# Attention by residue classes first, unit's columns fetched in phase A, attention norm in place, later norms by whole rows

## The chip, the core and the metric

The kernel runs on one core of one Trainium2 chip. The metric is the device time of one execution in microseconds; the median of the runs is compared. A second number is the time of one profiled execution, whose trace is read below.

## The reference, cut to what matters

Two sequences (prompt and sample) of 1024 tokens, 1024 features wide, pass through one encoder layer. Only what the change touches is shown.

```python
def encoder_layer(h, ...):
    z = rms_norm(h, g_mix) @ w_in                 # q, k, v (512 each) and u (512)
    att = attention_mixer(q, k, v, rel_bias)      # 8 heads of 64
    ssm = ssm_mixer(u, ...)                       # state-space part, then
                                                  # g * sigmoid(g @ w_glu + b_glu), the "unit"
    mix = concatenate([rms_norm(att, g_att_out), rms_norm(ssm, g_ssm_out)])
    h = h + mix @ w_out
    f = rms_norm(h, g_mlp)
    h = h + square(relu(f @ w_mlp1)) @ w_mlp2
    e = rms_norm(h, g_ple)
    h = h + sigmoid(e @ w_ple_gate) * (p_i @ w_ple_proj)
# at the end: rms_norm(h, g_final)
def attention_mixer(q, k, v, rel_bias):
    # three branches, windows (128, 512, 2048) at dilations (1, 4, 16); each gives
    # an output and the logarithm of its denominator, and these weigh the outputs
```

## The kernel before, in words

The kernel has three phases. **Phase A** norms the inputs, multiplies them by `w_in`, stores q, k, v and u in scratch memory, and runs the state-space part; the planner orders its instructions. **Phase B** (class `PhaseB`) is the attention, in an order written by hand for TensorE, VectorE and ScalarE: 64 steps, eight to a pair of heads, four pairs to a sequence. Each pair n has four blocks of contiguous windows (branch of dilation 1; tiles `q`, `k`, `v64`, statistics `sta`, output `ota`) and four blocks of residue classes modulo 4 (the two other branches together; tiles `qr`, `kr`, `vc`, statistics `stb`, output `otb`). `step(g)` does, for the block g and its neighbours, the scores (L783), bias and minimum (L807, VectorE), exponent (L815, ScalarE), transposes (L823), copies of these (L827) and products with v (L844), and copies the result with `put` (L852, L854). Before, blocks 0 to 3 of a pair are the windows and 4 to 7 the classes. `moved` (L888) exchanges `stb` between partitions into `sx` by four DMAs on GpSimd's queue; `joined` (L922) takes the statistics of both branches, works out their weights (L907 to L919), turns the outputs (L940), weighs them (L944), adds them (L947) and stores the tile `at` (L949). For the last pair `joined` runs after the loop, in one piece.

Between the steps, at four places of each, run other tasks as generators: `gelu` and `unit` of class `Glu` (the state-space part's end) and `att_norm` (L1096, the norm of the attention's output of the first sequence). `Glu` loads two columns of 512 values at its start (L965, L966), the unit's weights (L968), and `gelu` halves the columns on VectorE (L977) before it loads the first block of y (L982); GpSimd squares y (L986), VectorE goes on two steps later (L989). `att_norm` takes eight tiles of 128 tokens, one after another: product with gain and scale (L1114), four transposes (L1118), a high part by ScalarE (L1121) and the remainder by VectorE (L1122), each stored in scratch memory (L1125). The tag of the high parts has two buffers, that of the remainders one.

All loads and stores except `moved` go through SP's queue, in the order that the planner gives them. A new tile in a buffer waits until the tile before it has been read.

**Phase C** (class `PhaseC`) does `w_out`, the MLP and the PLE part for one sequence after the other, in split products (each operand as a high part and a remainder, three matmuls for one: L455 to L457; splits at L1168 and L1169, on ScalarE and on VectorE or GpSimd). `norm` (L1158) is called for four tiles at a time, twice before the MLP and twice before the PLE part, in each sequence. It uses `norm_to_act` (L523): squares and their sum on ScalarE (L519), the reciprocal root on VectorE (L419 to L428), the row scaled by it on ScalarE (L532), and for each of the 8 feature blocks of a group of two tiles two transposes (L537), a copy times the gain column on ScalarE (L540) and the remainder on VectorE (L541). Gains are columns (`gcol`, 1024 values of 4 bytes); the gain of the attention norm and the last norm are rows (`gvec`, tile `gbc`, one buffer). The last norm multiplies by row and scale in one VectorE operation (L1408).

Of the kernel before, what the change touches and what calls it, by code (L numbers as in the profile page):

```python
# [431 lines left out]
class Act:  # L432
# [12 lines left out]

    def rhs(self, k, th):
        return self.hi[k // 4, th][:, k % 4], self.lo[k // 4, th][:, k % 4]
# [75 lines left out]
def norm_to_act(nc, small, ps, tag, ident, act, T0, srcs, dst, gcol, nk, junks, group):  # L523

    r = rstd_rows(nc, small, srcs, nk * P, junks)
    last = None
    for t0 in range(0, len(srcs), group):
        ts = range(t0, min(t0 + group, len(srcs)))
        dsts = []
        for t in ts:  # L530
            dsts.append(dst(t))
            nc.scalar.activation(dsts[-1], srcs[t], AF.Copy, scale=r[:, t:t + 1])  # L532
        c = slice(P * ((T0 + t0) % 4), P * ((T0 + t0) % 4) + P * len(ts))
        for k in range(nk):
            pt = ps.tile([P, 4, P], F32, tag=tag, name="n_ps")
            for t in range(len(ts)):
                nc.tensor.transpose(pt[:, t], dsts[t][:, P * k:P * k + P], ident)  # L537
            hi, lo = (x[k // 4, T0 // 4][:, k % 4, c] for x in (act.hi, act.lo))
            pv = pt[:, 0:len(ts)].rearrange("p t c -> p (t c)")
            nc.scalar.activation(hi, pv, AF.Copy, scale=gcol[:, k:k + 1])  # L540
            last = nc.vector.scalar_tensor_tensor(lo, pv, gcol[:, k:k + 1], hi.bitcast(F32), op0=ALU.mult, op1=ALU.subtract)  # L541
    return last
# [127 lines left out]
class PhaseB:  # L670
# [6 lines left out]
    def __init__(self, nc, tc, ctx, early, ident, scr):  # L677
        self.nc, self.tc, self.ident, self.scr = nc, tc, ident, scr
        self.early = early

        def pool(name, bufs, **k):
            return ctx.enter_context(tc.tile_pool(name=name, bufs=bufs, reuse_waits="tile", **k))

        self.ld = [pool("Bl0", 1)]
        self.sp = pool("Bs", 7)
        self.ptp = pool("Bpt", 4)
        self.op = pool("Bo", 2)
        self.ap = pool("Ba", 1)
        self.sm = pool("Bsm", 2)
        self.ld.append(pool("Bl1", 1))  # L690
        self.ps_s = pool("Bps", 4, space=PSUM)
        self.ps_o = pool("Bpo", 1, space=PSUM)
        self.ps_t = pool("Bpt2", 2, space=PSUM)
        self.ps_x = pool("Bpx", 1, space=PSUM)
        self.tasks, self.busy, self.normed, self.place = [], False, False, 0
        self.pairs, self.pss, self.sbs, self.pts = {}, {}, {}, {}
# [22 lines left out]
    def load(self, n):  # L719
# [8 lines left out]
        with self.tc.high_priority(offset=FIRST_AHEAD if n == 0 else LOAD_AHEAD):  # L728
            q, k = (first([P, S], F32, "raw", nm) for nm in "qk")
            for t, nm in ((q, "zq"), (k, "zk")):  # L730
                nc.sync.dma_start(out=t, in_=scr[nm, s, p])
# [8 lines left out]
            v64 = ld.tile([P, 9, P], F32, tag="v64", name="v64")  # L740
            nc.sync.dma_start(out=v64, in_=zv.rearrange("(j m) e -> m j e", m=P))
            qr, kr = (ld.tile([P, 4, 256], F32, tag=nm, name=nm) for nm in ("qr", "kr"))
            for t, nm in ((qr, "zqr"), (kr, "zkr")):
                nc.sync.dma_start(out=t, in_=scr[nm, s, p])
            vc = ld.tile([P, 4, 2, P], F32, tag="vc", name="vc")
            for r in range(4):
                nc.sync.dma_start(out=vc[:, r], in_=zv[64:1088].rearrange("(f m r) e -> r m f e", m=P, r=4)[r])
        d = self.pairs[n] = dict(q=q, k=k, qr=qr, kr=kr, vc=vc, v64=v64, bt=bt)
# [12 lines left out]
    @staticmethod  # L761
    def cols(blk, u):
        return slice(64 if blk == u == 0 else 0, 192 if blk == 3 and u else 256)

    def scores(self, g):
# [6 lines left out]
        for u in range(2):  # L772
            w = self.cols(blk, u)
            for h in range(2):
                r = slice(64 * h, 64 * h + 64)
                if blk < 4:
                    i = 2 * b + u
                    ql = d["q"][r, P * i:P * i + P]
                    kr = d["k"][r, P * i - 64 + w.start:P * i - 64 + w.stop]
                else:  # L780
                    ql = d["qr"][r, b, P * u:P * u + P]
                    kr = d["kr"][r, b]
                self.nc.tensor.matmul(pss[h][:, u, w], ql, kr, start=True, stop=True)  # L783

    def stats(self, g, h, u):
        n, blk = g // 8, g % 8
        if blk < 4:
            st, i = self.some(n, "sta"), 2 * blk + u
            return [st[:, j, h, i:i + 1] for j in range(2)]
        st = self.some(n, "stb")  # L790
        return [st[:, blk - 4, j, h, u:u + 1] for j in range(2)]

    def reduced(self, g, h):
# [3 lines left out]
        for u in range(2):  # L797
            w = self.cols(blk, u)
            if blk < 4:
# [17 lines left out]
    def turn(self, g, h):  # L817
        sb = self.sbs.pop((g, h))
        self.pts[g, h] = pt = self.ps_t.tile([P, 4, P], F32, tag="pt", name="pt")
        for u in range(2):  # L820
            for kt in range(2):
                slot = 2 * u + kt if g % 8 < 4 else 2 * kt + u
# [7 lines left out]
    def values(self, g):  # L830
# [4 lines left out]
        if blk < 4:  # L835
# [12 lines left out]
    def put(self, g):  # L848
        n, blk = g // 8, g % 8
        b = blk % 4  # L850
        if blk < 4:
# [4 lines left out]
    def step(self, g, N=64):  # L856
# [18 lines left out]
        if on(g + 1):  # L875
            self.exponent(g + 1, 1)
            if g % 8 == 6:
                self.moved(g // 8)
# [43 lines left out]
    def joined(self, n, last=False):  # L922
# [3 lines left out]
        if not last:  # L926
            yield from self.at(3)
        ea, eb = yield from self.weights(n)
        at = self.ap.tile([P, 8, 2, 64], F32, tag="at", name="at")
# [24 lines left out]
class Glu:  # L954


    def __init__(self, nc, tc, ctx, io, ident, ones, scr, B):
# [6 lines left out]
        self.cols = self.one.tile([P, 8], F32, name="cols")  # L964
        nc.sync.dma_start(out=self.cols[:, 0:4], in_=io["b_glu"].rearrange("(f p) -> p f", p=P))  # L965
        nc.sync.dma_start(out=self.cols[:, 4:8], in_=io["g_ssm_out"].rearrange("(f p) -> p f", p=P))  # L966
# [5 lines left out]
    def gelu(self):  # L972
# [4 lines left out]
        nc.vector.tensor_scalar(self.cols, self.cols, 0.5, None, op0=ALU.mult)  # L977
# [118 lines left out]
def att_norm(nc, B, pool, g, io, scr, s):  # L1096
# [15 lines left out]
    for T, at in enumerate(ats):  # L1112
# [7 lines left out]
        hi, lo = (pool.tile([P, 4, P], F32R, tag="a" + x, name="ato", bufs=n) for x, n in (("h", 2), ("l", 1)))  # L1120
# [8 lines left out]
class PhaseC:  # L1129
# [23 lines left out]
    def gcol(self, src):  # L1153
        g = self.sm.tile([P, 8], F32, tag="gcol", name="gcol")
        self.nc.sync.dma_start(out=g, in_=src.rearrange("(k p) -> p k", p=P))
        return g

    def norm(self, h, gb, a, i):  # L1158

        a.half(i)  # L1160
        junks = [self.gp.tile([P, D], BF16, tag="junk", name="junk") for _ in range(4)]
        norm_to_act(self.nc, self.sm, self.pm1, "m1", self.ident, a, 4 * i, h[4 * i:4 * i + 4],
                    lambda t: self.sp.tile([P, D], F32, tag="s", name="ft"), gb, 8, junks, 2)
# [111 lines left out]
    def run(self, s, x, p, y, first=None):  # L1275
# [11 lines left out]
        gb = self.gcol(io["g_mlp"])  # L1287
# [13 lines left out]
        for ch in range(8):  # L1301
# [41 lines left out]
            else:  # L1343
# [26 lines left out]
                gb = self.gcol(io["g_ple"])  # L1370
# [42 lines left out]
def encoder_kernel(ctx, tc, io, y_prompt, y_sample):  # L1413
# [6 lines left out]
    m16 = c.tile([16, 16], F32, name="m16")  # L1420
    scr = {"u": tc.dram_tile([NG, 16, 8, 2, NCK], F32, name="u_scr"),
# [15 lines left out]
    with ExitStack() as ab:  # L1437
# [3 lines left out]
        with ExitStack() as as_:  # L1441
# [28 lines left out]
            M = Ssm(nc, tabs, ssmp, ps_gp, pk, ident, *ssm_in, m16, scr["u"], scr["y"])  # L1470
            M.step(0)
# [3 lines left out]
            A.qk(1, act, lambda p: M.step(5 + p))  # L1475
            A.v(1, act)
        right.close()
        with ExitStack() as bs:
# [3 lines left out]
            G = Glu(nc, tc, gs, io, ident, ones, scr, B)  # L1482
            bp = first = None
            for g in range(-3, 66):
                B.step(g)
                if bp is None and G.halves == 4 and g >= 40:
# [8 lines left out]
            place = 0  # L1495
# [3 lines left out]
            for _ in B.joined(7, True):  # L1499
                pass  # L1500
# [59 lines left out]
```

## Time and profile before

| what | us |
|---|---|
| median of 3 runs | 2791.08 (2786.3 to 2793.44) |
| the profiled execution | 2791.4 |
| its span, first to last instruction | 2789.6 |
| busy: TensorE | 2600.3 (93%) |
| busy: VectorE | 1583.1 (57%) |
| busy: ScalarE | 1190.6 (43%) |
| busy: GpSimd | 1129.4 (40%) |

In the rows, PE is TensorE, PEld its weight loads, DVE VectorE, ACT ScalarE, POOL GpSimd, SP the engine that issues the transfers. A row of a timeline has the start and the length in microseconds, the engine, the line, what was done, and in brackets how long the engine had been idle before and what released it. The granted clock is the share of TensorE's full speed.

### The profile page before, as it was taken

The page shows a single profiled execution, that of the slowest core. Times are in us where ns is not written, and L with a number is a line of the kernel's source. Part 1 is how long each engine was busy: PE and PEld are TensorE (multiplying, and loading weights), DVE is VectorE, ACT ScalarE, POOL GpSimd, SP SyncE. Part 2 cuts the span into 40 slices and gives each one's busy share as a digit, 9 for nine tenths or more (in the row PEclk, how much of TensorE's full clock was granted, in tenths as well). Part 3 has the DMA queues.
Part 4 walks back from the last instruction along what each step waited for, and adds up shares of the span by engine and source line. Part 5 has one row for each costly group of instructions (what it writes and reads, how often), then busy time and mean ns, then how long its engine had stood idle before and what let it go on. Part 6 is the DMA issues. An engine that isn't in the chain of part 4 may idle for free.

```text
span 2789.6 us, 33993 instructions
## 1 busy us (share of the span) xinstructions
PE 2600.3 (93%) x12206; PEld 2044.3 (73%) x12206; DVE 1583.1 (57%) x2923; ACT 1190.6 (43%) x2378; POOL 1129.4 (40%) x817
## 2 busy tenths in 40 slices
PE   6998878969997898999999999999999999999997
PEld 4866657755565686888788877787788888888776
DVE  4788775557776433475555574353356455457435
ACT  6433324236667444333333334533533333333452
POOL 1133343223331352464554464344344555455332
PEclk9999989989999898999999999999999999999999
DMA  8524453254447601122121222252111111111201
GB/s 280 150 78 121 157 165 115 91 173 150 150 130 267 195 31 32 48 72 72 42 68 42 64 91 64 84 204 72 53 54 53 46 42 57 61 53 46 72 16 61
DMA packets 271723, 266.67 MB, mean 96 GB/s; under 512 B 46897, under 2 KB 222001, under 8 KB 269505
## 3 DMA queue, kind: packets, MB, share of 16 engines
q1 hardware_dynamic: 270528, 264.36, 29.8%
q8 instruction: 96, 1.57, 0.2%
q14 instruction: 75, 0.61, 0.1%
q0 software_dynamic: 1024, 0.13, 0.0%
HBM read 194.55 MB, written 67.66 MB: 94 GB/s over the span
## 4 chain that ended last, share of the span: by engine, by line
PE 76%; DVE 12%; DMA 4%; ACT 4%; issue 2%; POOL 1%; SPq 0%; DVEq 0%; ACTq 0%; POOLq 0%
PE m L455 19%; PE m L457 19%; PE m L456 19%; PE glu L1014 2%; PE ag L455 2%; PE ag L457 2%; PE ag L456 2%; PE pss L783 1%; PE po L844 1%; PE n_ps L537 1%; PE pt L823 1%; DMA w<-in_w_mlp_dram 1%; PE s_pb L251 1%; DVE s_t L274 1%; ACT sb L815 1%
## 5 line engine op out<-in xcount | busy, mean ns | idle before, releaser
L1169 POOL TENSOR_TENSOR lo<-wr_b,hi 128x512 fp32r<-128x512 f32 x264 | 376.6, 1434 | 567.2 <-ACT hi L1168 552.5
L455 PE MATMUL m<-acth,hi 128*128 128x512 f32 x1024 | 403.9, 396 | 2.2 <-ACT hi L1168 2.2
L456 PE MATMUL m<-acth,lo 128*128 128x512 f32 x1024 | 403.2, 394 | 1.5 <-POOL lo L1169 1.5
L457 PE MATMUL m<-actl,hi 128*128 128x512 f32 x1024 | 403.1, 394 | 0.0
L1255 DVE TENSOR_TENSOR h<-h,m 128x512 f32<-128x512 f32 x448 | 288.3, 680 | 140.7 <-PE m L457 139.7
L456 PE MATMUL m<-hi,lo 128*128 128x512 f32 x912 | 354.8, 393 | 3.7 <-DVE lo L1169 3.7
L457 PE MATMUL m<-lo,hi 128*128 128x512 f32 x912 | 353.6, 394 | 0.3 <-POOL lo L1169 0.3
L455 PE MATMUL m<-hi 128*128 128x512 f32 x912 | 337.2, 396 | 4.8 <-DVE h L1255 3.6
L1168 ACT CAST hi<-wr_b 128x512 fp32r<-128x512 f32 x264 | 163.7, 621 | 410.1 <-PE m L456 375.9
L1169 DVE TENSOR_TENSOR lo<-hid,hi 128x512 fp32r<-128x512 f32 x200 | 185.1, 927 | 165.0 <-ACT hi L1168 165.0
L1169 POOL TENSOR_TENSOR lo<-w,hi 128x512 fp32r<-128x512 f32 x128 | 176.0, 1382 | 165.3 <-ACT hi L1168 164.0
L456 PEld LDWEIGHTS m<-acth,lo 128*128 128x128 f32 x1024 | 192.7, 188 | 47.9 <-POOL lo L1169 3.7
L455 PEld LDWEIGHTS m<-acth,hi 128*128 128x128 f32 x1024 | 192.7, 188 | 47.0 <-ACT hi L1168 2.8
L457 PEld LDWEIGHTS m<-actl,hi 128*128 128x128 f32 x1024 | 192.6, 188 | 45.1
L455 PE MATMUL m<-hi,acth 128*128 128x512 f32 x512 | 204.0, 401 | 7.8 <-issue 5.1
L456 PE MATMUL m<-hi,actl 128*128 128x512 f32 x512 | 205.5, 401 | 0.0
L455 PEld LDWEIGHTS m<-hi 128*128 128x128 f32 x912 | 171.8, 189 | 45.8 <-DVE h L1255 7.3
L456 PEld LDWEIGHTS m<-hi,lo 128*128 128x128 f32 x912 | 172.5, 189 | 42.3 <-DVE lo L1169 5.4
L457 PEld LDWEIGHTS m<-lo,hi 128*128 128x128 f32 x912 | 172.4, 189 | 38.7 <-POOL lo L1169 1.9
L457 PE MATMUL m<-lo,acth 128*128 128x512 f32 x512 | 194.8, 399 | 1.6 <-POOL lo L1169 1.6
L1319 ACT ACTIVATE hid<-m 128x512 f32<-128x512 f32 x128 | 76.1, 594 | 224.4 <-PE m L457 224.2
L455 PE MATMUL ag<-acth,whi 128*128 128x512 f32 x384 | 155.2, 405 | 3.6 <-ACT acth L540 3.6
(352 smaller groups left out, 4946.1 us busy)
## 6 DMA issues: line engine op xcount, KB each, us to landing
w<-in_w_mlp_dram SPq DMA_DIRECT2D x128, 256.0 KB, 2.9
wr_b<-in_w_mlp_dram SPq DMA_DIRECT2D x32, 1024.0 KB, 4.9
wraw<-in_w_in_dram SPq DMA_DIRECT2D x32, 512.0 KB, 4.9
mixa<-ato SPq DMA_DIRECT2D x32, 256.0 KB, 2.4
out_dram<-h SPq DMA_DIRECT2D x16, 512.0 KB, 2.7
v<-zv SPq DMA_DIRECT2D x8, 576.0 KB, 6.7
xt<-in_x_sample_dram SPq DMA_DIRECT2D x8, 512.0 KB, 7.9
xt<-in_x_prompt_dram SPq DMA_DIRECT2D x8, 512.0 KB, 5.9
```

What stands on the lines that cost most here:

```text
L251: nc.tensor.matmul(pb[:, k], w[:, i, g + k], u[:, g + k], start=True, stop=True)
L274: v.tensor_tensor_scan(flat(dst)[64:128, 0:n - 1][:, ::-1], flat(r0)[64:128, 0:n - 1][:, ::-1], flat(src)[64:128, 1:n][:, ::-1], 0.0, op0= ...
L455: nc.tensor.matmul(out, l[0], r[0], start=first, stop=False)
L456: nc.tensor.matmul(out, l[1], r[0], start=False, stop=False)
L457: nc.tensor.matmul(out, l[0], r[1], start=False, stop=last)
L537: nc.tensor.transpose(pt[:, t], dsts[t][:, P * k:P * k + P], ident)
L783: self.nc.tensor.matmul(pss[h][:, u, w], ql, kr, start=True, stop=True)
L1014: nc.tensor.matmul(o, self.w[:, k, P * f:P * f + P], gt[k][:, c], start=k == 0, stop=k == 3)
L1168: self.nc.scalar.copy(hi, src)
L1169: lo_eng.tensor_tensor(lo, src, hi.bitcast(F32), op=ALU.subtract)
L1255: eng.tensor_tensor(o, o, x, op=ALU.add)
L1319: nc.scalar.activation(z, o, AF.Relu)
```

## The change

1. In each pair the residue classes become blocks 0 to 3 and the windows blocks 4 to 7. The tiles of the classes are loaded first, `moved` runs at step 2 of a pair and not at step 6. For the last pair `joined` becomes a task of the last steps up to its weights, and goes on behind the loop.
2. The two columns of the unit are loaded on GpSimd's queue beside the state-space tables of phase A, and halved there.
3. `att_norm` writes the high parts in the place of the tile that was turned; the remainders get three buffers.
4. `norm` of phase C uses `norm_to_rows`: the row is multiplied by scale and gain row in one VectorE operation, and four feature blocks of one tile share a PSUM bank, one ScalarE copy and one VectorE subtraction. All its gains become rows in the one buffer `gbc`.

```diff
@@ class Act
+    def put(self, nc, kq, T, ps):
+        c = slice(P * (T % 4), P * (T % 4) + P)
+        hi, lo = self.hi[kq, T // 4][:, :, c], self.lo[kq, T // 4][:, :, c]
+        nc.scalar.copy(hi, ps)
+        return nc.vector.tensor_tensor(lo, ps, hi.bitcast(F32), op=ALU.subtract)
+def norm_to_rows(nc, small, ps, tag, ident, act, T0, srcs, dsts, gbc, nk=8, junks=None):
+    r = rstd_rows(nc, small, srcs, nk * P, junks or dsts)
+    last = None
+    for t, (src, dst) in enumerate(zip(srcs, dsts)):
+        nc.vector.scalar_tensor_tensor(dst, src, r[:, t:t + 1], gbc, op0=ALU.mult, op1=ALU.mult)
+        for kq in range(nk // 4):
+            pt = ps.tile([P, 4, P], F32, tag=tag, name="n_ps")
+            for i in range(4):
+                k = 4 * kq + i
+                nc.tensor.transpose(pt[:, i], dst[:, P * k:P * k + P], ident)
+            last = act.put(nc, kq, T0 + t, pt)
+    return last
@@ PhaseB.load
-            q, k = (first([P, S], F32, "raw", nm) for nm in "qk")
-            for t, nm in ((q, "zq"), (k, "zk")):
+            qr, kr = (first([P, 4, 256], F32, "raw", nm) for nm in ("qr", "kr"))
+            for t, nm in ((qr, "zqr"), (kr, "zkr")):
                 nc.sync.dma_start(out=t, in_=scr[nm, s, p])
             bt = first([P, 2, 640], F32, "bt", "bt")
...
-            v64 = ld.tile([P, 9, P], F32, tag="v64", name="v64")
-            nc.sync.dma_start(out=v64, in_=zv.rearrange("(j m) e -> m j e", m=P))
-            qr, kr = (ld.tile([P, 4, 256], F32, tag=nm, name=nm) for nm in ("qr", "kr"))
-            for t, nm in ((qr, "zqr"), (kr, "zkr")):
-                nc.sync.dma_start(out=t, in_=scr[nm, s, p])
             vc = ld.tile([P, 4, 2, P], F32, tag="vc", name="vc")
...
+            q, k = (ld.tile([P, S], F32, tag=nm, name=nm) for nm in "qk")
+            for t, nm in ((q, "zq"), (k, "zk")):
+                nc.sync.dma_start(out=t, in_=scr[nm, s, p])
+            v64 = ld.tile([P, 9, P], F32, tag="v64", name="v64")
+            nc.sync.dma_start(out=v64, in_=zv.rearrange("(j m) e -> m j e", m=P))
@@ PhaseB: scores, stats, reduced, turn, values, put
-        if blk < 4:
+        if blk >= 4:
@@ PhaseB.step
-            if g % 8 == 6:
+            if g % 8 == 2:
                 self.moved(g // 8)
@@ PhaseB.joined
-        if not last:
-            yield from self.at(3)
+        yield from self.at(3)
         ea, eb = yield from self.weights(n)
+        while last and not self.ended:
+            yield
@@ Glu
-        self.cols = self.one.tile([P, 8], F32, name="cols")
-        nc.sync.dma_start(out=self.cols[:, 0:4], in_=io["b_glu"].rearrange("(f p) -> p f", p=P))
-        nc.sync.dma_start(out=self.cols[:, 4:8], in_=io["g_ssm_out"].rearrange("(f p) -> p f", p=P))
+        self.cols = cols
...
-        nc.vector.tensor_scalar(self.cols, self.cols, 0.5, None, op0=ALU.mult)
@@ att_norm
-        hi, lo = (pool.tile([P, 4, P], F32R, tag="a" + x, name="ato", bufs=n) for x, n in (("h", 2), ("l", 1)))
+        hi = at.bitcast(F32R).rearrange("p (f c) -> p f c", f=4)
+        lo = pool.tile([P, 4, P], F32R, tag="al", name="ato", bufs=3)
@@ PhaseC.norm
+        fts = [self.sp.tile([P, D], F32, tag="s", name="ft") for _ in range(4)]
         junks = [self.gp.tile([P, D], BF16, tag="junk", name="junk") for _ in range(4)]
-        norm_to_act(self.nc, self.sm, self.pm1, "m1", self.ident, a, 4 * i, h[4 * i:4 * i + 4],
-                    lambda t: self.sp.tile([P, D], F32, tag="s", name="ft"), gb, 8, junks, 2)
+        norm_to_rows(self.nc, self.sm, self.pm1, "m1", self.ident, a, 4 * i, h[4 * i:4 * i + 4], fts, gb, 8, junks)
@@ PhaseC.run
-        gb = self.gcol(io["g_mlp"])
+        gb = self.gvec(io["g_mlp"], D)
...
-                gb = self.gcol(io["g_ple"])
+                gb = self.gvec(io["g_ple"], D)
@@ encoder_kernel
+            for i, nm in enumerate(("b_glu", "g_ssm_out")):
+                nc.gpsimd.dma_start(out=cols[:, 4 * i:4 * i + 4], in_=io[nm].rearrange("(f p) -> p f", p=P))
...
             A.qk(1, act, lambda p: M.step(5 + p))
+            nc.vector.tensor_scalar(cols, cols, 0.5, None, op0=ALU.mult)
...
                 B.step(g)
+                if g == 62:
+                    B.tasks.append(B.joined(7, True))
...
-            place = 0
+            B.ended, place = True, 0
             while B.tasks:
                 B.tasks_at(place % 4)
                 place += 1
-            for _ in B.joined(7, True):
-                pass
```

## Rows read from the trace of the kernel before

**Rows 1.** Page, slices of the span: granted clock of TensorE in tenths.
```profile
PEclk9999989989999898999999999999999999999999
```
**Rows 2.** Timeline, start of phase B: columns, y, and who waits for them.
```profile
598.74 0.38 SPq L965 DMA_DIRECT2D cols<-in_b_glu_dram  x1
...
600.50 0.43 SPq L968 DMA_DIRECT2D wglu<-in_w_glu_dram  x1
...
602.01 17.12 SPq L982 DMA_DIRECT2D yt<-y_scr  x3
603.98 0.17 DVE L977 TENSOR_SCALAR cols<-cols 128x8 f32<-128x8 f32 x1 [13.78 <-DMA cols<-in_g_ssm_out_dram]
...
611.47 1.89 POOL L986 TENSOR_TENSOR ge<-yt 128x1024 f32<-128x1024 f32 x1 [35.43 <-DMA yt<-y_scr]
...
613.39 1.23 DVE L989 SCALAR_TENSOR_TENSOR ge<-ge,yt 128x1024 f32<-128x1024 f32 x1 [5.37 <-POOL ge L986]
```
**Rows 3.** Stretches: us; busy PE, PEld, DVE, ACT, POOL; clock; DMA share; GB/s.
```profile
606.00:611.00 5.00, 4.82 (x24) 3.09 (x24) 2.03 (x12) 1.07 (x5) 0.00 (x0) 0.50 1.08 359
```
**Rows 4.** Timeline and chain of waits (second row) around the attention norm's stall.
```profile
899.24 20.16 SPq L1125 DMA_DIRECT2D mixa<-ato  x8
...
901.87 7.99 DMA mixa<-ato
...
909.97 0.69 DVE L1122 TENSOR_TENSOR ato<-n_ps,ato 128x512 fp32r<-128x512 f32 x1 [12.14 <-DMA mixa<-ato]
...
918.32 0.69 DVE L1122 TENSOR_TENSOR ato<-n_ps,ato 128x512 fp32r<-128x512 f32 x1 [1.10 <-ACT ato L1121]
```
**Rows 5.** Timeline, end of phase B and first matmul of phase C.
```profile
925.45 6.01 SPq L1150 DMA_DIRECT2D gbc<-in_g_att_out_dram  x1
...
933.87 0.37 SPq L949 DMA_DIRECT2D att<-at  x1
...
934.57 0.62 ACT L854 COPY otb<-po 128x256 f32<-128x256 f32 x1 [1.19 <-PE po L844]
...
936.18 0.83 DVE L907 TENSOR_TENSOR m<-sta,sx 128x16 f32<-128x16 f32 x1 [3.10 <-DMA sx<-stb]
...
940.47 0.69 DVE L944 TENSOR_TENSOR at<-px,ea 128x512 f32<-128x512 f32 x1
...
941.86 0.77 PE L455 MATMUL m<-hi,acth 128*128 128x512 f32 x1 [5.08 <-issue]
```
**Rows 6.** Line L949 from 900 to 960 us: time to landing of its stores.
```profile
DMA to landing us min/median/max: 3.9/3.9/4.0
```
**Rows 7.** Stretches: second MLP norm of either sequence, PLE norms of the first.
```profile
1047.60:1065.10 17.50, 13.43 (x63) 9.41 (x61) 9.86 (x20) 14.92 (x28) 4.92 (x3) 0.81 0.00 0
1974.70:1992.10 17.40, 13.19 (x62) 9.26 (x60) 9.85 (x20) 14.84 (x28) 4.92 (x3) 0.85 0.00 0
1733.50:1755.60 22.10, 18.09 (x84) 13.97 (x84) 12.34 (x33) 15.46 (x28) 5.58 (x4) 0.98 0.31 117
```
**Rows 8.** Groups from 1047.6 to 1065.1 us: busy us, mean ns, idle before.
```profile
L540 ACT ACTIVATE acth<-n_ps,gcol 128x256 fp32r<-128x256 f32 x15 | 6.4, 478 | 2.1 <-PE n_ps L537 2.1
L541 DVE SCALAR_TENSOR_TENSOR actl<-n_ps,gcol,acth 128x256 fp32r<-128x256 f32 x14 | 6.1, 480 | 3.7 <-ACT acth L540 3.7
L532 ACT ACTIVATE ft<-h,nr 128x1024 f32<-128x1024 f32 x4 | 4.5, 1142 | 2.4 <-DVE nr L428 2.4
...
L1202 POOL TENSOR_TENSOR wr_b<-wr_b,t 128x1024 f32<-128x1024 f32 x1 | 2.4, 2395 | 0.1
```
**Rows 9.** Single lines over the span: ns minimum, median, maximum; first and last start.
```profile
L1408 DVE SCALAR_TENSOR_TENSOR h<-h,nr,gbc x16: 1279/1285/2324, 1821.2 to 2784.3; 128x1024 f32<-128x1024 f32 x16
L1121 ACT CAST ato<-n_ps x8: 585/586/589, 873.2 to 917.7; 128x512 fp32r<-128x512 f32 x8
L1122 DVE TENSOR_TENSOR ato<-n_ps,ato x8: 691/692/692, 873.8 to 918.3; 128x512 fp32r<-128x512 f32 x8
L894 POOL DMA_DIRECT2D sx<-stb x32: 547/569/710, 632.0 to 931.5; - x32
```

More of the change, by code (lines that the diff above doesn't have):

```diff
@@ L694, in __init__ @@
         self.ps_x = pool("Bpx", 1, space=PSUM)
-        self.tasks, self.busy, self.normed, self.place = [], False, False, 0
+        self.tasks, self.busy, self.normed, self.ended, self.place = [], False, False, False, 0
         self.pairs, self.pss, self.sbs, self.pts = {}, {}, {}, {}
@@ L762, in cols @@
     def cols(blk, u):
-        return slice(64 if blk == u == 0 else 0, 192 if blk == 3 and u else 256)
+        return slice(64 if blk == 4 and not u else 0, 192 if blk == 7 and u else 256)
     def scores(self, g):
@@ L786, in stats @@
         n, blk = g // 8, g % 8
-        if blk < 4:
-            st, i = self.some(n, "sta"), 2 * blk + u
+        if blk >= 4:
+            st, i = self.some(n, "sta"), 2 * (blk - 4) + u
             return [st[:, j, h, i:i + 1] for j in range(2)]
         st = self.some(n, "stb")
-        return [st[:, blk - 4, j, h, u:u + 1] for j in range(2)]
+        return [st[:, blk, j, h, u:u + 1] for j in range(2)]
     def reduced(self, g, h):
@@ L798, in reduced @@
             w = self.cols(blk, u)
-            if blk < 4:
+            if blk >= 4:
                 bias = bt[:, h, 0:256][:, ::-1][:, w]
@@ L821, in turn @@
             for kt in range(2):
-                slot = 2 * u + kt if g % 8 < 4 else 2 * kt + u
+                slot = 2 * u + kt if g % 8 >= 4 else 2 * kt + u
                 self.nc.tensor.transpose(pt[:, slot], sb[:, u, P * kt:P * kt + P], self.ident)
@@ L834, in values @@
         po = self.ps_o.tile([P, 256], F32, tag="po", name="po")
-        if blk < 4:
+        if blk >= 4:
             seq = [(d["v64"][:, 2 * b + 1], slice(1, 3), slice(0, 256)), (d["v64"][:, 2 * b], slice(0, 1), slice(0, 128)),
@@ L850, in put @@
         b = blk % 4
-        if blk < 4:
+        if blk >= 4:
             self.nc.scalar.copy(self.some(n, "ota")[:, 256 * b:256 * b + 256], self.po)
@@ L954, with __init__ @@
 class Glu:
-    def __init__(self, nc, tc, ctx, io, ident, ones, scr, B):
+    def __init__(self, nc, tc, ctx, io, ident, ones, scr, B, cols):
         self.nc, self.io, self.ident, self.ones, self.scr, self.B = nc, io, ident, ones, scr, B
@@ L1151, in gvec @@
         return g[:, 0:n]
[L1153 to L1156, printed above, removed]
     def norm(self, h, gb, a, i):
         a.half(i)
+        fts = [self.sp.tile([P, D], F32, tag="s", name="ft") for _ in range(4)]
         junks = [self.gp.tile([P, D], BF16, tag="junk", name="junk") for _ in range(4)]
-        norm_to_act(self.nc, self.sm, self.pm1, "m1", self.ident, a, 4 * i, h[4 * i:4 * i + 4],
-                    lambda t: self.sp.tile([P, D], F32, tag="s", name="ft"), gb, 8, junks, 2)
+        norm_to_rows(self.nc, self.sm, self.pm1, "m1", self.ident, a, 4 * i, h[4 * i:4 * i + 4], fts, gb, 8, junks)
     def split(self, pool, tag, src, shape, lo_eng):
@@ L1420, in encoder_kernel @@
     m16 = c.tile([16, 16], F32, name="m16")
+    cols = c.tile([P, 8], F32, name="cols")
     scr = {"u": tc.dram_tile([NG, 16, 8, 2, NCK], F32, name="u_scr"),
@@ L1481, in encoder_kernel @@
             gs = ExitStack()
-            G = Glu(nc, tc, gs, io, ident, ones, scr, B)
+            G = Glu(nc, tc, gs, io, ident, ones, scr, B, cols)
             bp = first = None
```

## Prediction

> **What bounds the kernel now.** TensorE does the work that sets the end, and it is slowed where it waits: the slices of the page give the granted clock first [rows 1]. It is 9 (0.9 or more) nearly everywhere, and 8 in single slices, so I look for single holes and not for a slow engine. I read the views in this order. The timeline of phase B (the attention, up to 942 us) shows three places where VectorE stands in its queue for a transfer and TensorE behind it. At the start VectorE waits 13.78 us for the unit's columns and, two steps later, 5.37 us for GpSimd, which itself waited for the first block of y [rows 2]. Near the end it waits 12.14 us for a store of the attention norm [rows 4]. At the very end it waits 3.10 us for the exchanged statistics, and TensorE begins phase C 5.08 us late [rows 5]. Phase C I read by stretches: around the second MLP norm of each sequence ScalarE is busy 14.92 of 17.50 us and the granted clock falls to 0.81 and 0.85; around the PLE norms ScalarE is busy 15.46 of 22.10 us [rows 7]. The profiled execution took 2791.4 us (span 2789.6 and 1.8 around it), the median of the three runs 2791.08; I subtract from 2791.4 and the two differ by nothing that matters.
>
> **Part 1, columns and order at the start of phase B.** Removed from SP's queue: two column loads. From the issue of the first to the issue of the next transfer, the unit's weights, SP spent 600.50 - 598.74 = 1.8 us on them [rows 2]. Removed from VectorE's queue: the small scaling at 603.98 with its wait of 13.78 us. That wait isn't gained. VectorE would do steps 0 and 1 some 13.8 us sooner and then stand before L989, because that needs GpSimd's square of y (1.89 us, started at 611.47) and that needs the y load, issued at 602.01 as the next in SP's queue. So the next late thing is the y load. It stands behind the other pair's tiles in transfer queues that are full (1.08 of their share from 606 to 611 us, [rows 3]), and taking two tiny loads away brings it forward by the 1.8 us of issue, nothing if the transfers alone set its landing, and some 5 us if it also slips ahead of the second pair's loads (the whole 5.37 us wait). I take 2, the issue row being the nearest. The columns now come over GpSimd's queue in phase A: two issues; the nearest row is the exchange's, 0.57 us each [rows 9], so 1.1 us of GpSimd, which is not TensorE's supplier there; 0 to 1 us, taken as 0. The residue classes first only trade which of the tiles (qr, kr, vc against q, k, v64) are loaded first. The count of matmuls per pair is unchanged, the early pool holds two tiles as before, and the later four blocks' tiles have four steps to land: 0, and if that cover went, one landing.
>
> **Part 2, attention norm in place.** L1122 of tile 5 waited 12.14 us because its lo tile had one buffer and the store of tile 4's was late: issued at 901.87 after the queue had been held, landed 7.99 us later, at 909.86 [rows 4]. With three buffers tile 5 and 6 don't wait. Tile 7 takes tile 4's buffer. In the trace it follows tile 5 by 918.32 - 909.97 = 8.35 us; without the wait tile 5 would be at 897.83, tile 7 at 906.2, and it would find the store 3.7 us short of landed. The gain is between 12.14 - 3.7 = 8.4 and 12.1; I take 9, the store being late for reasons that stay. ScalarE's copy now writes into the tile that was transposed, which is read out by then: 0.
>
> **Part 3, the end of phase B.** The exchange of statistics for the last pair moves four steps earlier, and the weights are worked out inside the last steps. It drops the 3.10 us wait and the small operations from 936.18 to 940.47 from the chain [rows 5]. Next late: the last copy of TensorE's results ends at 934.57 + 0.62 = 935.2, and the tile `at` has one buffer, whose last store was issued at 933.87 and landed 3.9 us later, at 937.8 [rows 5, 6]. So VectorE starts at 937.8 and not 940.47: 2.7 us; 5.3 if the store were no bound; 0 if the store, which now follows sooner on the norm's loads, lands later by as much. I take 2.7. The issues of the exchange stand earlier in GpSimd's queue behind one ScalarE exponent of the same step; the other seven moves cost nothing as VectorE asks for them a step after the pair ends. In SP's queue the gain row of the MLP norm (512 KB, broadcast) takes the place of a 4 KB column load. A broadcast issue in this place held SP 6.01 us waiting for its memory [rows 5], before the `at` store; it did so before, too. Taken as 0, at most 6. The other gain rows now wait until the one before is used up, since they share one buffer; SP has long idle times in phase C: 0.
>
> Phase B gives 2 + 9 + 2.7 = 13.7 us (from 0 + 8.4 + 0 = 8 to 5 + 12.1 + 5.3 = 22).
>
> **Part 4, the norms of phase C**, eight calls, four tiles each. Per call ScalarE loses 4 scalings of 1.142 us and 16 copies of 0.478 and gains 8 copies of 0.586 us [rows 8, 9]: 12.2 becomes 4.7. VectorE loses 16 operations of 0.480 us and gains 4 products of 1.285 (L1408, same shape) and 8 subtractions of 0.692 us: 7.7 becomes 10.7. The transposes stay 32. The first MLP norm hides behind the second half's products, before and after. The second one doesn't: in its stretch VectorE was busy 9.86 us, 6.1 of it in this norm [rows 7, 8], so it becomes 9.86 - 6.1 + 5.1 + 5.5 = 14.4 us, while ScalarE falls from 14.92 to 14.92 - 10.9 + 4.7 = 8.7. The stretch took 17.5; bound by VectorE it takes 14.4 at best, a gain of 3.1. L1408 also ran at 2.324 us when GpSimd was at work; with all four so slow, 18.6 us, a loss of 1.1. GpSimd is busy 4.92 of 17.50 us there, so I lean to the fast end: 2 us. If the clock stayed at its higher level, up to 3 us more. The same stretch recurs in the other sequence [rows 7]. Around the PLE norms VectorE has 12.34 of 22.1 us; with the new norm's 10.7 in and the old one's 7.7 out in whole or not at all it is between 15.3 and 23.0. So the gain is at best like the MLP's 3, the loss at worst 23.0 - 22.1 = 0.9; 2 again, once per sequence. Four places of 2 us: 8, from -4 (two of -1.1, two of -0.9) to 18 (two of 3.1 + 3, two of 3).
>
> **The sum**: 13.7 + 8 = 21.7; 2791.4 - 21.7 = 2770 us.
>
> **Rivals.** (a) The norms only change engines: VectorE's longer queue eats what ScalarE's shorter one frees. Then phase B alone pays, 2791.4 - 13.7 = 2778. For it: the products at 2.3 us; against: ScalarE's share in rows 7. (b) Everything opens, y slips forward, no wait for tile 4's store, the clock comes back: 22 + 18 = 40 us, 2752. (c) The transfers set phase B: what landed during the stall must still land, the y load doesn't move and `at` is stored behind it, so the waits re-form a step later, and of part 2's 8.4 us about half is given back before phase C, nothing comes of parts 1, 3 and 4, and about 4 us are left: 2787, no change that can be told. For it: queues at 1.08; against: the store of tile 4 isn't needed by anyone else. (d) Slower: each product waits for a whole operation of GpSimd (L1202, 2.395 us, [rows 8]) since both read two tiles of SBUF. Then VectorE needs 14.4 + 4 x 2.4 = 24.0 us where there were 17.5, 6.5 lost at each of four places, 26 in all; less the 13.7 of phase B, 12 slower: 2804. It decides from a delay of 1.6 us per product on; the rows show 1.04 (2.324 against 1.285), which speaks against it.
>
> The Trainium skill's page "SBUF — State Buffer", section "SBUF: two separate sides", says of this that a VectorE operation with two SBUF inputs and a GpSimd operation that reads SBUF take one shared port pair in turn, whoever starts first holding it for the whole instruction. By that rule (d) would hold wherever a product starts behind L1202; the rows of L1408 agree that products get longer, by 1.04 us and not by 2.4.
>
> **How the numbers follow.** Chances: forecast 0.45 (2762 to 2778 its own range), (a) 0.22, (b) 0.12, (c) 0.13, (d) 0.08. A measurement of this kernel tells about 0.3%, 8.4 us, from no change. Faster by more: forecast, (a) and (b), 0.79; within it: (c), 0.13; slower: (d), 0.08. The range 2752 to 2787 takes in (a), (b)'s and (c)'s figures and leaves out (d) and the halves of (b) and (c) beyond them, about 0.2.
>
> **What would show it.** Part 1: no wait at L977's place, and L989 still waiting for GpSimd with its end near 611 and not near 600. Part 2: no long wait at L1122's successor, or one of a few us at tile 7. Part 3: the weights before the last copy, TensorE's gap before phase C about 2 us instead of 5. Part 4: ScalarE under 10 us in the stretch of the second MLP norm, VectorE the engine that TensorE's transposes wait for, products between 1.28 and 2.33 us. The forecast is wrong if y lands much sooner, if the planner of phase C orders TensorE's queue differently and opens new holes, or if a gain row holds SP ahead of weights.

## The result, and the profile after

| what | before | after |
|---|---|---|
| median, us | 2788.69 (2785.66 to 2793.44) | 2759.38 (2755.36 to 2760.73) |
| ratio, 95% interval | | 0.9891 (0.9872 to 0.991) |
| the profiled execution, its span, us | 2791.4, 2789.6 | 2758.93, 2757.2 |
| phase A, to the first score of the attention | 586.4 | 589.4 |
| phase B, to the first matmul of `w_out` | 355.4 | 353.6 |
| phase C, to the end of the span | 1847.7 | 1814.1 |

The kernel is 29.3 us faster, at 2759 where 2770 was predicted, within the range of 2752 to 2787. The last three rows, of one profile each, say at once that this isn't the sum that was predicted: phase B was to give 13.7 us and gave 1.8, phase A lost 3.0, and phase C was to give 8 and gave 33.6. That the time lies as near the forecast as it does is luck, as the experiments show: more than half of the gain came from an effect that the prediction didn't have.

The page of the kernel after, its span and the granted clock by slices (before: [rows 1]):

```profile
span 2757.2 us, 33930 instructions
...
PEclk9999998989999999999999999999999999999999
```

The start of phase B after the change, timeline (start, length, engine, line; in brackets the idle time before and what ended it; lines of the changed kernel):

```profile
589.43 0.92 PE L804 MATMUL pss<-kr,qr 64*128 64x256 f32 x6 [0.93 <-ACT zv L679]
...
603.59 19.05 SPq L1001 DMA_DIRECT2D yt<-y_scr  x3
613.40 3.74 POOL L1005 TENSOR_TENSOR ge<-yt 128x1024 f32<-128x1024 f32 x2 [34.37 <-DMA yt<-y_scr]
615.32 2.90 DVE L1008 SCALAR_TENSOR_TENSOR ge<-ge,yt 128x1024 f32<-128x1024 f32 x1 [17.88 <-POOL ge L1005]
...
620.25 1.09 PE L844 MATMUL pt<-ident,sb 128*128 128x128 f32 x4 [18.46 <-DVE pT L848]
```

The wait for the columns is gone, and L1008 (L989 before) stands 17.88 us where the two waits were 13.78 + 5.37 [rows 2]. Counted from the first score, y is there 613.40 - 589.43 = 23.97 us in; before it was 611.47 - 586.42 = 25.05. But both blocks of y are there by then, GpSimd squares them on end (3.74 us), and L1008 takes 2.90 us beside the second square instead of 1.23. TensorE stands 18.46 us in one piece.

The attention norm and the end of phase B:

```profile
920.86 0.69 DVE L1142 TENSOR_TENSOR ato<-n_ps,att 128x512 fp32r<-128x512 f32 x1 [5.12 <-DMA mixa<-ato]
...
923.58 1.12 PE L844 MATMUL pt<-ident,sb 128*128 128x128 f32 x4 [4.43 <-DVE pT L848]
...
938.15 0.36 SPq L971 DMA_DIRECT2D att<-at  x1
...
941.68 0.69 DVE L966 TENSOR_TENSOR at<-px,ea 128x512 f32<-128x512 f32 x1 [1.94 <-DMA att<-at]
...
943.07 0.47 PE L461 MATMUL m<-hi,acth 128*128 128x512 f32 x1 [2.58 <-issue]
```

The wait of 12.14 us [rows 4] is one of 5.12, for the eighth tile; TensorE's gap before phase C is 2.58 us instead of 5.08 [rows 5], and what comes last there is the landing of the `at` store.

The norms' places in phase C (us; busy PE, PEld, DVE, ACT, POOL; clock; DMA share; GB/s): the second MLP norm, the PLE norms of the first sequence, the second MLP norm of the second (before: [rows 7]):

```profile
1049.30:1068.40 19.10, 13.12 (x61) 9.44 (x60) 17.72 (x25) 9.58 (x17) 6.02 (x3) 0.91 0.06 15
1719.00:1741.00 22.00, 19.75 (x97) 15.69 (x96) 20.57 (x31) 10.30 (x19) 10.76 (x7) 1.00 0.33 110
1960.50:1979.50 19.00, 12.96 (x60) 9.31 (x59) 17.71 (x25) 9.57 (x17) 6.02 (x3) 0.91 0.10 29
```

ScalarE is down to 9.6 us, VectorE is full: 17.7 of 19 us. The MLP norm's stretch isn't shorter than the 17.5 us of before. At the PLE norms TensorE does 97 operations in 22 us where it did 84.

None of this makes 33.6 us. This does: a stretch in which TensorE is wholly busy at full clock in both kernels, in the MLP of the second sequence. First the kernel before, then after (same columns):

```profile
2000.00:2600.00 600.00, 600.00 (x2612) 489.66 (x2611) 305.99 (x405) 217.36 (x375) 291.04 (x185) 1.00 0.16 50
```

```profile
2000.00:2600.00 600.00, 600.00 (x2657) 497.01 (x2656) 319.32 (x423) 226.26 (x393) 301.78 (x191) 1.00 0.17 52
```

In 600 us TensorE does 2657 operations and not 2612, without a gap, with the same clock: 225.8 ns from one to the next instead of 229.7. (Some transposes lie in either stretch, 16 after and 2 before, 108 ns each; they don't make the 45.) The change touches no instruction of this stretch. Laid against the addresses that the two programs give their tiles, the starts of successive matmuls in this stretch of the kernel before fall into two kinds: where the moving tile lies 32 bytes beyond a multiple of 64 and the weight tile being loaded lies on one, or the other way round, they are about 233 ns apart (868 of them); where both lie alike, about 228 (1739). After, nearly all are 226 or 227 ns apart. Before, the left-hand pools of phase C began on a multiple of 64 bytes and the right-hand ones 32 beyond. The tile of the unit's columns (8 values, 32 bytes per partition), which the change puts among the constants, shifts the left side by 32 bytes, and all lie alike.

### The profile page after: what moved, and what is told of

Read it like the earlier page. It is cut to its first block, busy times and chain, and to the rows that moved or that the text cites. A ratio compares the mean times of both kernels' runs of the same rounds, so it can differ in the third digit from the quotient of the medians.

```text
span 2757.2 us, 33930 instructions
## 1 busy us (share of the span) xinstructions
PE 2568.5 (93%) x12206; PEld 2040.7 (74%) x12206; DVE 1631.9 (59%) x2891; ACT 1139.8 (41%) x2282; POOL 1138.5 (41%) x819
## 4 chain that ended last, share of the span: by engine, by line
PE 75%; DVE 14%; DMA 4%; ACT 3%; issue 2%; POOL 1%; SPq 0%; DVEq 0%; ACTq 0%; POOLq 0%
PE m L461 19%; PE m L462 19%; PE m L463 19%; PE ag L462 2%; PE ag L461 2%; PE ag L463 2%; PE glu L1033 2%; PE pss L804 1%; PE pt L844 1%; PE po L865 1%; DMA w<-in_w_mlp_dram 1%; ACT sb L836 1%; PE s_pb L251 1%; PE n_ps L561 1%; DVE s_t L274 1%
```

## Experiments

Theory: the 33.6 us of phase C are two things, the place of the tiles (some 22 us, an estimate of 3 ns for each of 7000 matmuls) and the norms (some 11). Main rival: the new norms relieve the engines, and matmuls run freer for it. For phase B: the y load's place in SP's queue, against the transfers themselves.

| kernel | median, us | less than before of its round, us | phase A | phase B | phase C | TensorE operations, 2000 to 2600 us |
|---|---|---|---|---|---|---|
| before | 2788.69 | | 586.4 | 355.4 | 1847.7 | 2612 |
| after | 2759.38 | 29.3 | 589.4 | 353.6 | 1814.1 | 2657 |
| e1 before, pad left | 2770.12 | 18.5 | 589.7 | 355.5 | 1829.0 | 2657 |
| e2 after, columns 64 bytes | 2778.43 | 10.1 | 588.5 | 348.0 | 1837.2 | 2617 |
| e3 before, norms | 2780.83 | 7.7 | 586.7 | 353.9 | 1838.6 | 2614 |
| e4 before, pad right | 2770.19 | 18.4 | 589.1 | 357.6 | 1827.1 | 2657 |
| e5 after, old norms | 2773.27 | 14.9 | 588.7 | 349.0 | 1831.0 | 2656 |
| e6 after, y asked later | 2770.59 | 17.6 | 589.0 | 355.4 | 1824.1 | 2654 |
| e7 after, exchange at step 6 | 2758.40 | 29.8 | 589.6 | 353.5 | 1817.1 | 2656 |
| e8 after, four remainders | 2758.67 | 29.5 | 590.6 | 349.4 | 1816.8 | 2655 |
| e9 after, y by GpSimd | 2755.60 | 35.5 | 589.0 | 343.0 | 1823.0 | 2655 |
| e10 e9 and e8 | 2752.42 | 38.7 | 589.0 | 340.5 | 1825.7 | 2656 |
| e11 before, pad and norms | 2764.07 | 27.0 | 588.9 | 357.9 | 1819.0 | 2657 |
| e12 before, pad and part 2 | 2767.98 | 23.1 | 586.5 | 349.1 | 1828.8 | 2656 |

The stages are of one profile each. The kernel before was timed again in each round, with a median between 2788.2 and 2791.1 us; the third column goes by it, and medians of different rounds compare to some 3 us only.

**e1, a pad of 32 bytes.** To the kernel before:

```diff
+    pad = c.tile([P, 8], F32, name="pad")
+    nc.gpsimd.memset(pad, 0.0)
```

> The kernel before with one unused tile of 32 bytes per partition among the constants; nothing else. Theory (place of the tiles): the built program puts the left-hand pools of phase C at a multiple of 64 bytes and the right-hand ones 32 bytes beyond one; matmuls whose moving tile and weight tile lie differently start 233 ns apart, the others 227 to 228. The pad shifts the left side by 32 bytes, as the tile of columns does in the changed kernel, so all lie alike: 2789 - 22 = 2767 us, and in the wholly busy stretch from 2000 to 2600 us about 2655 matmuls instead of 2612. Rival (the new norms relieve the engines and the matmuls run freer): an unused tile does nothing, 2789 us and 2612 matmuls.

2770.12, ratio 0.9937 (0.9915 to 0.9958): 18.5 us for a tile that nobody reads. In the profile phase C is 18.7 us shorter (1847.7 to 1829.0); phase A is 3.3 longer, which stays open. The row of the long stretch:

```profile
2000.00:2600.00 600.00, 600.00 (x2657) 497.04 (x2656) 313.33 (x416) 223.90 (x388) 294.26 (x187) 1.00 0.17 51
```

**e2, the columns' tile widened.** To the kernel after:

```diff
-    cols = c.tile([P, 8], F32, name="cols")
+    cols = c.tile([P, 16], F32, name="cols")[:, 0:8]
```

> The changed kernel with the tile of the unit's columns widened from 32 to 64 bytes per partition, the second half unused. Theory (place): the left side moves back to a multiple of 64 bytes while the right stays 32 beyond, so the 22 us are lost again: 2759 + 22 = 2781 us. Rival (norms): 2759 us.

2778.43 (0.9962, 0.995 to 0.9974): 19 of the 29 us are lost again.

```profile
2000.00:2600.00 600.00, 600.00 (x2617) 489.92 (x2616) 309.55 (x411) 219.72 (x380) 290.94 (x184) 1.00 0.16 50
```

**e3, the norms alone**, part 4 of the change in the kernel before.

> The kernel before with part 4 alone, the norms of phase C by whole rows. The tiles stay where they were. Theory (place): the norms give only what the gaps and half-clock stretches give, some 11 us: 2778 us; matmuls from 2000 to 2600 us stay at about 2612. Rival (norms do it all): 33 us, 2756, and about 2655 matmuls.

2780.83 (0.9977, 0.9965 to 0.9988): 7.7 us, close to the 8 of the prediction, and 2614 operations in the long stretch. The main rival falls.

**e4, the pad on the other side.** To the kernel before:

```diff
+    rp = ctx.enter_context(tc.tile_pool(name="rpad", bufs=1, side="right"))
+    pad = rp.tile([P, 8], F32, name="pad")
+    nc.gpsimd.memset(pad, 0.0)
```

> The kernel before with the unused tile of 32 bytes on the right-hand side instead, so that all tiles of phase C lie at a multiple of 64 bytes. Theory (moving and weight tile must lie alike): as with the pad on the left, 2767 us. Rival (lying 32 bytes beyond a multiple of 64 is itself the fast place): no gain, 2789 us or more.

2770.19, as e1. What counts is that moving and weight tile lie alike, on 64 or beside it.

**e5, the change without its norms**: part 4 taken out of the kernel after.

> The changed kernel with the norms of phase C of before, so parts 1 to 3 and the columns' 32-byte tile, whose place stays. Theory: the norms were worth 8 to 11 us, the rest of phase C's gain is the tiles' place: 2759 + 9 = 2768 us. Rival (place and norms are one thing): 2780 or more.

2773.27 (0.9948, 0.9931 to 0.9965): 13.9 us above the kernel after, more than the 7.7 of e3. What goes beyond the norms is one place, the end of the first sequence's MLP. 60 us of e5, of the kernel after, and of e7, which runs the operations of TensorE, VectorE, ScalarE and GpSimd in the very order of the kernel after:

```profile
1590.00:1650.00 60.00, 53.80 (x208) 40.41 (x208) 51.45 (x75) 19.57 (x35) 37.89 (x24) 0.91 0.28 84
```

```profile
1600.00:1660.00 60.00, 55.31 (x240) 43.68 (x239) 53.96 (x76) 23.87 (x42) 42.27 (x27) 1.00 0.34 103
```

```profile
1600.10:1660.10 60.00, 57.06 (x238) 45.34 (x237) 52.99 (x76) 23.71 (x42) 42.58 (x27) 0.94 0.34 103
```

All three begin with the same gap of 1.6 us at TensorE; behind it the clock fell to half in e5 and in e7 and didn't in the kernel after. The fall alone isn't what costs: e7 does 238 operations where the kernel after does 240, e5 only 208. The lines of e5 are the same here, but the planner put them into another order. Timeline of e5, and one row of the kernel after:

```profile
1613.45 0.69 DVE L1284 TENSOR_TENSOR u<-u,m 128x512 f32<-128x512 f32 x1 [3.07 <-PE m L463]
...
1631.38 0.50 PE L462 MATMUL m<-hi,lo 128*128 128x512 f32 x1 [2.95 <-DVE lo L1189]
...
1632.45 0.74 DVE L570 SCALAR_TENSOR_TENSOR att<-att,nr,gbc 128x512 f32<-128x512 f32 x1
```

```profile
1621.42 0.75 DVE L570 SCALAR_TENSOR_TENSOR att<-att,nr,gbc 128x512 f32<-128x512 f32 x1
```

VectorE's product L570, of the second sequence's attention norm, comes 26.6 us behind the gap and not 6.6; before it VectorE stands 3.07 us for a matmul, and TensorE later 2.95 us for a remainder. The 14 kernels have two orders here. From the gap to the 400th MLP matmul behind it the nine with the order of the kernel after take 96.6 to 99.1 us (after 96.6, e7 97.1, e1 99.1), the five others 102.5 to 104.7 (e5 103.7, e6 104.6, e9 104.7, e10 104.2, e12 102.5). In seven of the nine the clock fell as well, and in all five others, so what the second order would cost at full clock isn't shown. So some 7 of the 13.9 us of e5 go with the order, at a place ahead of the PLE norms, and about 7 are left for the norms.

**e11, pad and norms without parts 1 to 3.**

> The kernel before with the unused 32-byte tile on the left and part 4, the norms by whole rows; nothing of parts 1 to 3. Theory (place and norms are the whole change, parts 1 to 3 give nothing that reaches the end): 2770 - 11 = 2759, as the changed kernel. Rival (parts 1 to 3 are worth the 5 us that some profiles of the attention show): 2764 or more.

2764.07 (0.9901, 0.9886 to 0.9917): 6.1 us below e1 (8.5 by the third column), 4.7 above the kernel after (2.3), whose interval it overlaps. With e1 and e5 (2770.12 and 2773.27, the same comparison without the norms) parts 1 to 3 give between -3 and 5 us; the -3 has in it that e5 takes 4.6 us longer than e1 at the place above.

**e6, VectorE asks for y four steps later.** To the kernel after:

```diff
                 nc.gpsimd.tensor_tensor(e, z, z, op=ALU.mult)
+                if s == f == 0:
+                    for _ in range(4):
+                        yield from B.at(3)
```

> The changed kernel; VectorE asks for GpSimd's first square of y four steps later, all loads issued as before. Theory (the y load alone makes the start stall, since VectorE stands in order before L1008): TensorE's gap of 18.46 us at 602 us shrinks to what the second pair's tiles leave, under 6 us, and the attention is 10 us or more ahead by 710 us; what of it reaches the end is 5 to 10 us: 2751. Rival (the transfers set the pace, or the unit's later end moves the attention norm against the end of phase B): the gap forms again a step or two later and the end gains nothing: 2759.

2770.59, 11 us slower than the kernel after. The stall shrank from 18.46 to 6.84 us, and step 12 began 13 us sooner, as expected; but the unit and the norm run as tasks of the steps, all four steps later now, and by step 36 the lead was 2.4 us; phase B took 355.4 us. The other 10 us are in phase C, 8 of them at the place of e5's rows, where this kernel has e5's order.

**e9, y on GpSimd's queue.** To the kernel after:

```diff
-                nc.sync.dma_start(out=yt, ...)
+                (nc.gpsimd if s == 0 and f < 2 else nc.sync).dma_start(out=yt, ...)
```

> The changed kernel; the first two loads of y are issued by GpSimd and not in SP's queue, where they stand behind the loads of the first two pairs and of the unit's weights. Theory (the place of the y load in SP's queue makes the start stall, and the gain stays because the unit's work keeps its steps, which it did not when VectorE asked later): y lands some 8 us sooner, TensorE's gap of 18.46 us at 602 us shrinks to under 9, phase B is 8 us shorter, 2751. Rival (the transfers are full anyway, and the tiles of the pairs come as much later as y comes sooner): phase B as long as in the changed kernel, 2759.

2755.60 (0.9879, 0.9864 to 0.9894), 3.8 us below the kernel after (6.2 by the third column), with overlapping intervals. Timeline of e9:

```profile
595.60 1.89 POOL L1005 TENSOR_TENSOR ge<-yt 128x1024 f32<-128x1024 f32 x1 [5.37 <-DMA yt<-y_scr]
...
597.52 1.22 DVE L1008 SCALAR_TENSOR_TENSOR ge<-ge,yt 128x1024 f32<-128x1024 f32 x1 [0.45 <-POOL ge L1005]
...
610.27 2.00 DVE L1012 SCALAR_TENSOR_TENSOR g<-ge,yt 128x1024 f32<-128x1024 f32 x1 [9.64 <-DMA zv<-zv]
...
614.31 1.94 PE L844 MATMUL pt<-ident,sb 128*128 128x128 f32 x8 [9.24 <-DVE pT L848]
```

y comes 17.8 us sooner (595.60 against 613.40), and 15.2 of these are the issue (588.41 against 603.59): the queue held it, not the transfers. A new wait follows: L1012 stands 9.64 us for a last store of phase A (`zv`). Phase B is 10.6 us shorter, and here the lead stays to its end. In the profile 12 us of lead, phase A's 0.4 included, last until 1616 us; then 8 go at the place of e5's rows. From `w_out` on, this is the only place where the operations of TensorE, VectorE and ScalarE stand in another order than in the kernel after.

**e8, four buffers for the remainders**; the squares' unread output shares one of them.

```diff
-    junk = pool.tile([P, 512], BF16, tag="junk", name="junk", bufs=1)
+    junk = pool.tile([P, 512], F32, tag="al", name="junk", bufs=4)
...
-        lo = pool.tile([P, 4, P], F32R, tag="al", name="ato", bufs=3)
+        lo = pool.tile([P, 4, P], F32R, tag="al", name="ato", bufs=4)
```

> The changed kernel with four buffers for the attention norm's remainders instead of three (the squares that nobody reads go into one of them, for room). Theory (the eighth tile of the norm waits for the store of a remainder): the wait of 5.12 us at 920.86 is gone, TensorE's gap of 4.43 us with it, and 3 to 4 us reach the end: 2755.5. Rival (the stores follow one another in SP's queue and the last loads of phase C's first operands wait for them): nothing, 2759.

2758.67, no difference. The wait for the eighth tile is gone, and at the end of phase B one for `at` has grown from 1.94 to 8.37 us:

```profile
938.53 0.69 DVE L966 TENSOR_TENSOR at<-px,ea 128x512 f32<-128x512 f32 x1 [8.37 <-DMA att<-at]
```

**e10, e9 and e8 together.**

> The kernel of the run before this one, with four buffers for the attention norm's remainders as well. Theory: the two waits are independent, 2750. Rival (whatever the attention gains is taken back at its end): 2757 to 2759.

2752.42 (0.9862, 0.9845 to 0.9878), the lowest median of all, 7 us below the kernel after, though the two intervals of the ratio still overlap; against e9 alone (3.2 us) it isn't told apart. Phase B ends 13 us sooner than in the kernel after, with the wait for `at` (6.32 us) as its last.

**e7, the exchange of statistics at step 6 again.**

```diff
-            if g % 8 == 2:
+            if g % 8 == 6:
```

> The changed kernel with the exchange of statistics issued at step 6 of a pair, as before, though the classes are done by then. Theory (the early exchange collides on GpSimd with the joining of the pair before, and VectorE's small operations wait for it): the attention's steps 36 to 48, which lost 9 us, get back about 4, the end of phase B pays 2.5 for the late exchange; about 2757. Rival (the exchange's place does not matter; the loss is the loads' order): steps 36 to 48 unchanged, 2761.

2758.40, and no answer: the planner orders GpSimd's instructions by what they need, and put the exchange where it was (of pair 4 at 803.89 us, in the kernel after at 803.76). So it is a repetition of the kernel after: phase B 353.5 and 353.6 us, step by step alike.

**e12, part 2 alone on e1.**

> The kernel before with the unused 32-byte tile on the left and part 2 alone, the attention norm's high parts in place with three buffers for the remainders. Theory (part 2 takes 12.14 us of waiting down to some 5, and in the order of before this reaches the end): phase B 349 instead of 355.5 us, 2770 - 7 = 2763. Rival (the wait forms again at the end of phase B, or with tile 7): 2770.

2767.98 (0.9924, 0.9911 to 0.9937), 2.1 us below e1 (4.6 by the third column), within the noise, with e5's order at the end of the MLP; phase B 349.1 us, 6.4 shorter. The eighth tile waits here too:

```profile
910.53 0.69 DVE L1123 TENSOR_TENSOR ato<-n_ps,att 128x512 fp32r<-128x512 f32 x1 [4.83 <-DMA mixa<-ato]
```

## Where the prediction was right, and where wrong

The range held, the sum did not: 21.7 us were summed, and 18.5 came from a term that it didn't have (e1), 6 to 9 from the norms (e11 on e1, e3, e5 less the 7 us of its order), and between -3 and 5 from parts 1 to 3, which were to bring 13.7. Without the place of the tiles the kernel stands at 2778 (e2), 10 us below the kernel before and less than half of the sum; that 2759 came out near 2770 is luck.

**Part 1**: 2 us predicted, nothing measured. The step itself was read rightly: the columns' wait wasn't gained, VectorE stood at L1008 for y, and y was 1.1 us sooner of the 1.8 of issue. Missing was that the two squares now stand on end and L1008 runs beside the second, 1.7 us longer, and ends 1.08 us behind it (the mechanism of rival (d), below). The larger slip: the prediction weighed the 1.8 us of issue, the full transfers and a slip ahead of the second pair's loads, at most 5 us, and took the rest of SP's queue as given. After, 16 loads and two stores are issued between the last store of y (588.92) and its first load (603.59); e9 shows that there the 18 us lie.

**Part 2**: 9 predicted. The residual wait of 3.7 us at the eighth tile came as told, at 5.12; 12.14 - 5.12 = 7.0 at the place, 6.4 by e12. Right mechanism, 2 us too large.

**Part 3**: 2.7 predicted, TensorE's gap fell by 2.5, bound by the `at` store as told.

**The sum of phase B** failed on a term that was put at zero: the residue classes first. Starts of the steps, counted from the phase's first score:

| | step 36 | step 48 | step 60 | first `w_out` matmul |
|---|---|---|---|---|
| before | 218.1 | 270.0 | 334.4 | 355.4 |
| after | 216.7 | 278.0 | 329.1 | 353.6 |
| e2 | 213.9 | 272.5 | 323.9 | 348.0 |
| e5 | 214.5 | 274.5 | 324.8 | 349.0 |
| e12 (windows first) | 218.4 | 270.5 | 321.9 | 349.1 |

Those with the classes first lose 7 to 9 us against the old order between steps 36 and 48, and gain 1 to 4 before. Two places of the kernel after:

```profile
803.76 2.21 POOL L915 DMA_DIRECT2D sx<-stb  x4
...
804.81 3.59 DVE L935 TENSOR_TENSOR dn<-ea,sta 128x16 f32<-128x16 f32 x1
...
805.93 2.42 POOL L1048 TENSOR_TENSOR sq<-sq 128x1024 f32<-128x1024 f32 x1
...
863.72 0.63 ACT L1126 ACTIVATE junk<-att 128x512 bf16<-128x512 f32 x1 [6.17 <-DMA att<-att]
...
865.51 1.12 PE L865 MATMUL po<-pT,v 128*64 128x256 f32 x4 [4.64 <-ACT ota L873]
```

Two stretches, the kernel before and after, steps 36 to 48:

```profile
804.50:856.40 51.90, 44.60 (x360) 30.87 (x358) 41.94 (x169) 39.72 (x134) 19.72 (x21) 1.00 0.74 247
```

```profile
806.10:867.40 61.30, 49.56 (x368) 34.79 (x366) 45.70 (x169) 39.80 (x134) 19.61 (x17) 0.88 0.72 221
```

Of the 9.4 us lost TensorE is idle for some 5 (11.7 against 6.6 us of gaps); for the rest it is busy longer, 49.56 against 44.60 us with eight operations more, at a granted clock of 0.88 and not 1.00. The exchange (L915) now falls into the steps in which the pair before is joined; GpSimd's sum of squares comes behind it, and an operation of VectorE that elsewhere takes 0.17 us ends with it, 3.59 us long. And the attention norm's loads now stand in SP's queue behind the next pair's, so ScalarE waits 6.17 us for them where it waited 3.7. "The other seven moves cost nothing" was the step; whether this collision or the order of the loads is most of it wasn't settled, since e7 didn't move what it should. The collision isn't all: in e6, whose unit comes four steps later, that operation takes 0.17 us, and steps 36 to 48 still take 57.7 us, though e6 moves other work into them as well.

**Part 4**: 8 predicted; 7.7 by e3, 6 to 9 by e11, about 7 by e5 without its order. The size was right, the places weren't: nothing at the MLP norms, where VectorE was put at 14.4 to 18.6 us and is busy 17.7, and some 6 us at the PLE norms of either sequence (5.5 and 6.3 in the profiles of e3 and before, by the start of the same matmuls ahead of the place and behind it). There TensorE had waited for ScalarE's scaled row. All transposes of the later norms, busy us, mean ns, idle before and its causes, before and after:

```profile
L537 PE MATMUL n_ps<-ident,ft 128*128 128x128 f32 x256 | 48.1, 301 | 16.1 <-ACT ft L532 9.3 <-DVE actl L541 6.7
```

```profile
L561 PE MATMUL n_ps<-ident,ft 128*128 128x128 f32 x256 | 35.6, 283 | 13.2 <-DVE actl L450 11.1 <-DVE ft L556 1.9
```

**The rivals.** (a) fell: the norms pay. (c) describes phase B best: the waits re-formed, and about as much was left as it said. (b)'s time was nearest, but none of its reasons: y didn't slip forward. (d) didn't decide, yet its mechanism is there, and 1.04 us was no bound for it. Timeline of the second MLP norm after:

```profile
1054.85 2.73 POOL L1217 TENSOR_TENSOR wr_b<-wr_b,t 128x1024 f32<-128x1024 f32 x1
...
1055.25 3.42 DVE L556 SCALAR_TENSOR_TENSOR ft<-h,nr,gbc 128x1024 f32<-128x1024 f32 x1
...
1062.18 1.27 DVE L556 SCALAR_TENSOR_TENSOR ft<-h,nr,gbc 128x1024 f32<-128x1024 f32 x1
```

L1217 ends at 1057.58 and the product 1.09 us later: it waited for the whole rest of GpSimd's operation. The 2.324 us of L1408 [rows 9] were such a rest too, of an operation of 1.28 us that had begun 0.04 us before, and no row there said how long GpSimd's operation still ran. The Trainium skill's page "SBUF — State Buffer", section "SBUF: two separate sides", states just this, that whoever holds the shared port pair holds it for the whole instruction; the trace agrees, and it should have set the bound. It hit 16 of the 32 products, those that began while an operation of GpSimd ran: each ended 1.08 or 1.09 us behind that operation. Of 14 of these operations less than 1.3 us was left; the products took 1.44 to 3.42 us, the others 1.27 to 1.29.

**Not settled**: why the clock falls behind the same gap at the end of the MLP in some executions and not in others, e7 and the kernel after, with the same order, among them; it cost 0.5 us there. And the 3 us of phase A, which moved between 586.4 and 590.6 us without a pattern that fits the pads or the columns' loads.

## What to carry to other kernels

Count TensorE's operations in a wholly busy stretch before and after: if the count moves and neither the clock nor the kind of operations does, no wait explains the time, and one unused tile of 32 bytes tests whether the place of the tiles does. Of a wait at an engine that takes its work in order, ask what the next late thing stands behind in its own queue: moving the load gave 10 us of phase B, asking for it later gave none. A gain in one stage is believed when the end of the kernel shows it: where a planner orders the instructions, an edit in one phase can change the order in another, and here 7 to 8 us went with that. So compare the order of each engine's operations before a difference is given to the edit or to the clock.

## What the runs showed of the hardware

Matmuls of 128x512 whose moving tile and next weight tile differ by 32 bytes modulo 64 in their addresses start about 233 ns apart, others 227 to 228, at granted clock 1.00: 18.5 us of this kernel, had by a pad on either side (e1, e4) and lost by widening a tile (e2). Only the distance of 32 bytes was tried.

A product of VectorE with two tiles of SBUF that begins while an operation of GpSimd runs ends 1.08 or 1.09 us behind it, however much of that was left: 16 of 32 of L556 after (1.44 to 3.42 us) and 7 of 16 of L1408 before (2.28 to 2.32); those that began alone or before GpSimd took 1.27 to 1.29.
